# A hybrid decoder layer on one core: summed weights written over the raw ones, and another order of the gate/up steps

## The chip, the core and the metric

The kernel runs on one core of one Trainium2 chip. Time is the device time of one execution in microseconds (us); the number that counts is the median of several runs. The engines are TensorE (PE: matrix products, with weight loads shown apart as PEld), VectorE (DVE), ScalarE (ACT), GpSimd (POOL) and SyncE (SP, which here only starts transfers). Each has a queue of its own and takes its instructions strictly in the order in which they stand; an instruction whose input isn't ready holds up all that stands behind it on its engine.

## The reference

One decoder layer on 256 tokens of width 2048, all in float32:

```python
u = rmsnorm(h, ln1_w)
lru_x, lru_g, q, k, v, ret_g = split(u @ w_in)           # 2048 -> 6 x 1024
y = concat(rg_lru(conv(lru_x)) * gelu(lru_g), retention(q, k, v, ret_g))
h = h + y @ w_out                                         # 2048 -> 2048
u = rmsnorm(h, ln2_w)
ff = silu(u @ w_ffn_gate) * (u @ w_ffn_up)                # 2048 -> 5632, twice
h = h + ff @ w_ffn_down                                   # 5632 -> 2048
out = rmsnorm(h, final_norm_w)
```

The change lies in the last three lines, above all in `u @ w_ffn_gate` and `u @ w_ffn_up`.

## The kernel before

**Products in three parts.** Every float32 operand is split into a high part (rounded to the matrix engine's format, a copy on ACT, L102) and a low part (source minus high part, on DVE, L103). A product is then three matmuls: high by high, high by low, low by high (`three`, L656; the lines are L659, L660 and L661). The weights are split on the fly: a 128x1024 float32 tile `raw` (512 KB) is loaded, ACT writes `wh`, DVE writes `wl`, PE uses both. There are 5 `raw` buffers, and 4 each of `wh` and `wl`.

**A quad.** The gate/up weights come as quads: one quad is 256 rows of the left factor (two halves of 128, for two token tiles of 128: a11, a12, a21, a22) by a gate tile and an up tile of 512 columns (b11, b21 for gate, b12, b22 for up), in two loads: first half b11 and b12, second half b22 and b21. A plain quad costs eight products (`EIGHT`). A summed quad costs seven (`SEVEN`), Strassen's way, with weight sums t1 = b11 + b12, t2 = t1 + b22, t3 = b12 + b22, t4 = t2 + b21 on DVE, and sums s1 to s4 of the left factor made once (`Left`, L521). Results gather in PSUM banks c11, c21 (gate) and c12, c22 (up). There are two sets of four banks, `bank` and `aux`; column blocks take them in turn (`room`, L652).

**Column blocks.** Gate/up has 11 blocks j of 512 columns, each with 8 quads. In block 0 (`gate_up_first`) the quads numbered in SUMMED_FIRST are summed. In the blocks 1 to 10 (`gate_up`) the three quads numbered in SUMMED are worked in two steps, so that three of them share the additions on the results. A *shared* step, done while the block before is still running, computes the four products with b11, t2, t1, t3 into the banks of the next block; behind the last of the three, a few additions (L760 to L765, `p1`, `p`, `q`) mix those banks. A *direct* step, in its own block, loads the second half of the quad again and adds the three products with b21, t4 and b22; t4 is kept from the shared step. The other five quads are *plain* steps. So in steady state one block has five plain steps of 24 matmuls, three shared steps of 12 and three direct steps of 9: 183 matmuls and 19 loads.

**After a block** `ffn_post` (L811) applies the gate: tanh on ACT (L820), two products on DVE for each token tile (L821, L825), then eight transposes on PE (`turn`, L826, tile `ft`) and two copies on ACT to `ff`. `resid_tok` (L580) transposes the residual in some blocks (tile `ht`).

**Down** (`down_block`) has two blocks of 22 quads, five of them in each summed (SUMMED_DOWN) through the same `Quad.load`.

**What sets the order.** `program` is a list of steps; loads run three ahead of the step that needs them (AHEAD, L1067); `defer` puts late work off by a number of steps. That is the order in which the code is written; a list scheduler then sets the final order of each engine's queue when the kernel is built, and gives out the buffers. Queues are therefore fixed before the kernel runs.

## Time and profile before

| | |
|---|---|
| three runs | 1128.27, 1135.15, 1137.65 us; median 1135.15 |
| profiled execution | 1135.66 us; its span, first to last instruction, 1133.9 us |
| granted TensorE clock, mean | 0.996 |
| input projections, retention, output projection | 0 to about 388 us of the span |
| gate/up: block 0 | about 388 to 441 us |
| gate/up: blocks 1 to 10 | about 441 to 900 us |
| down and final norm | about 900 to 1134 us |

All positions below are microseconds from the start of the span of that one execution. In a row of the timeline stand the start, the time taken, the engine, the line of the kernel, the operation, output<-input, the size, how many, and in brackets the idle time of the engine just before it with what ended it. In a row of stretches stand, for each engine, busy microseconds and in brackets the number of instructions, then the granted clock, the share of the transfer engines' time, and GB/s. A matmul's recorded length overlaps the next one's: the distance between two starts is what one costs PE.

### The profile page before, as it was taken

To read this page: it belongs to the slowest core of one execution; us is meant where nothing else is said; L and a number is where in the kernel's file an instruction comes from. 1 tells how busy PE (TensorE), PEld (TensorE's weight loads), DVE (VectorE), ACT (ScalarE), POOL (GpSimd) and SP (SyncE) were. 2 spreads that over 40 slices of the span, in tenths; PEclk is the share of its full clock that TensorE was granted. 3 is DMA by queue.
4 is the path that set the end of the run, shared out by engine and by line. 5 is a ranking of instruction groups with operands and counts; after the bars stand their busy time and mean duration, and the time that the engine had idled before them with its cause. 6 is when DMAs were issued, how large, how long until landed. Compare 5 with 4: busy or idle time off the path is not lost.

```text
span 1133.9 us, 14754 instructions
## 1 busy us (share of the span) xinstructions
PE 1100.2 (97%) x5298; PEld 915.2 (81%) x5298; DVE 906.6 (80%) x1274; ACT 639.0 (56%) x877; POOL 57.4 (5%) x64
## 2 busy tenths in 40 slices
PE   9999999999999999999998999989999999999996
PEld 7888888888888977877876877767777888888885
DVE  7797799968777889778787787778876799777774
ACT  7766644478666556555555455554545665554553
POOL 0602220000000000000000000000000000020001
PEclk9999999999999999999999999999999999999999
DMA  9765565645655466667566575665757456746572
GB/s 326 236 196 167 177 232 168 196 156 169 215 192 186 146 208 241 217 211 240 196 231 228 176 239 182 234 223 184 246 186 256 160 183 209 245 140 219 199 240 76
DMA packets 66538, 230.47 MB, mean 203 GB/s; under 512 B 7584, under 2 KB 7968, under 8 KB 66464
## 3 DMA queue, kind: packets, MB, share of 16 engines
q1 hardware_dynamic: 65664, 227.43, 60.5%
q0 software_dynamic: 512, 1.57, 0.4%
q8 instruction: 41, 0.67, 0.2%
q10 hardware_dynamic: 288, 0.52, 0.1%
q14 instruction: 33, 0.27, 0.1%
HBM read 227.40 MB, written 2.10 MB: 202 GB/s over the span
## 4 chain that ended last, share of the span: by engine, by line
PE 60%; DVE 18%; DMA 15%; issue 4%; ACT 2%; DVEq 0%; SPq 0%; ACTq 0%
PE fm L143 15%; DMA raw<-in_w_gu 15%; DVE wl L103 10%; PE c L660 9%; PE c L661 8%; PE c L659 8%; PE fm L144 8%; PE tm L159 3%; PE tm L160 3%; PE tm L161 3%; ACT wh L102 2%; DVE raw L721 1%; DVE sum L717 1%; DVE raw L719 1%; PE p L659 1%
## 5 line engine op out<-in xcount | busy, mean ns | idle before, releaser
L103 DVE TENSOR_TENSOR wl<-raw,wh 128x1024 fp32r<-128x1024 f32 (+1 forms) x384 | 461.6, 1217 | 112.9 <-ACT wh L102 108.4
L102 ACT CAST wh<-raw 128x1024 fp32r<-128x1024 f32 (+1 forms) x384 | 390.4, 1032 | 274.2 <-DMA raw<-in_w_gu 60.3
L660 PE MATMUL c<-wl,ah 128*128 128x512 f32 x788 | 309.8, 395 | 14.8 <-DVE wl L103 14.7
L661 PE MATMUL c<-wh,al 128*128 128x512 f32 x788 | 306.7, 391 | 0.0
L659 PE MATMUL c<-wh,ah 128*128 128x512 f32 x788 | 261.4, 393 | 1.4 <-ACT wh L102 1.4
L660 PEld LDWEIGHTS c<-wl,ah 128*128 128x128 f32 x788 | 148.1, 188 | 53.8 <-DVE wl L103 24.3
L143 PE MATMUL fm<-u,wh 128*128 128x512 f32 x512 | 180.2, 396 | 0.0
L659 PEld LDWEIGHTS c<-wh,ah 128*128 128x128 f32 x788 | 147.8, 188 | 35.0 <-ACT wh L102 4.6
L661 PEld LDWEIGHTS c<-wh,al 128*128 128x128 f32 x788 | 148.1, 188 | 29.6
L144 PE MATMUL fm<-u,wl 128*128 128x256 f32 x512 | 144.1, 282 | 0.0
L102 ACT CAST wh<-sum 128x1024 fp32r<-128x1024 f32 x54 | 56.2, 1051 | 118.3 <-DVE sum L717 75.0
L143 PEld LDWEIGHTS fm<-u,wh 128*128 128x128 f32 x512 | 96.1, 188 | 22.0
L144 PEld LDWEIGHTS fm<-u,wl 128*128 128x128 f32 x512 | 97.0, 190 | 0.2
L143 PE MATMUL fm<-y,wh 128*128 128x512 f32 x224 | 78.8, 398 | 0.0
L103 DVE TENSOR_TENSOR wl<-sum,wh 128x1024 fp32r<-128x1024 f32 x54 | 65.3, 1222 | 6.4 <-ACT wh L102 6.2
L144 PE MATMUL fm<-y,wl 128*128 128x256 f32 x224 | 62.6, 281 | 0.0
L940 POOL TENSOR_TENSOR htok<-htok,fw 128x512 f32<-128x512 f32 (+1 forms) x7 | 10.9, 1573 | 934.2 <-ACT junk L938 934.2
L659 PE MATMUL c<-wh,sh 128*128 128x512 f32 x132 | 49.8, 403 | 5.8 <-ACT wh L102 5.5
L716 DVE TENSOR_TENSOR sum<-raw 128x512 f32<-128x512 f32 x30 | 20.7, 691 | 42.9 <-DMA raw<-in_w_gu 42.9
L660 PE MATMUL c<-wl,sh 128*128 128x512 f32 x132 | 52.1, 395 | 0.0
L661 PE MATMUL c<-wh,sl 128*128 128x512 f32 x132 | 52.0, 394 | 0.0
L143 PEld LDWEIGHTS fm<-y,wh 128*128 128x128 f32 x224 | 42.0, 188 | 10.0
(264 smaller groups left out, 1349.6 us busy)
## 6 DMA issues: line engine op xcount, KB each, us to landing
raw<-in_w_gu SPq DMA_DIRECT2D x206, 512.0 KB, 4.7
raw<-in_w_down SPq DMA_DIRECT2D x88, 512.0 KB, 4.4
raw<-in_w_out SPq DMA_DIRECT2D x32, 512.0 KB, 3.8
raw<-in_w_lx SPq DMA_DIRECT2D x16, 512.0 KB, 4.9
raw<-in_w_k SPq DMA_DIRECT2D x16, 512.0 KB, 3.7
raw<-in_w_q SPq DMA_DIRECT2D x16, 512.0 KB, 4.3
raw<-in_w_rg SPq DMA_DIRECT2D x16, 512.0 KB, 3.7
raw<-in_w_lg SPq DMA_DIRECT2D x16, 512.0 KB, 4.0
```

What stands on the lines that cost most here:

```text
L102: act.copy(out=dst_h, in_=src)
L103: v.tensor_tensor(out=dst_l, in0=src, in1=dst_h.bitcast(F32), op=ALU.subtract)
L143: pe.matmul(ps, wh, hl, start=first, stop=False)
L144: pe.matmul(ps[:, :S], wl, hl[:, :S], start=False, stop=last)
L159: pe.matmul(ps, ah, wh, start=first, stop=False)
L160: pe.matmul(ps, ah, wl, start=False, stop=False)
L161: pe.matmul(ps, al, wh, start=False, stop=last)
L659: pe.matmul(p, ah, bh, start=first, stop=False, skip_group_check=onto)
L660: pe.matmul(p, ah, bl, start=False, stop=False, skip_group_check=onto)
L661: pe.matmul(p, al, bh, start=False, stop=last, skip_group_check=onto)
L716: v.tensor_tensor(out=ta[:, :512], in0=b11, in1=b12, op=ALU.add)
L717: v.tensor_tensor(out=ta[:, 512:], in0=ta[:, :512], in1=b22, op=ALU.add)
```

## The change

**The sums are written over the raw weights.** A new function `add` puts t1 into the place of b11, t3 into that of b12, t2 into that of b22 and t4 into that of b21. The `sum` tiles, which took buffers of the `raw` pool (two for each summed quad, one for each shared step), are gone. Since b11, b22 and b21 are overwritten, they are split first where they are needed raw: in `Quad.load` the pair b22, b21 is split ahead of the sums; in `Shared.load` b11 is split as soon as the first half is there. The shared step's pairs change with that: b11 and t2 share one `wh`/`wl` pair, filled by two splits of 512 columns at different times, t1 and t3 share another, filled by one split of 1024. Before, t1 and t2, and b11 and t3, went together, in two splits of 1024.

**The steps of a block stand in another order.** Before, a block was: direct, direct, direct, plain, plain, shared, plain, shared, plain, shared, plain. Now: plain, plain, shared, direct, plain, shared, direct, plain, shared, direct, plain. The shared steps still belong to the next block.

**Smaller parts.** The quads worked in the Strassen way are now 2, 3 and 4 (before 1, 3 and 5), and in block 0 only quad 2 (before 1 and 3). A plain quad's eight products now start with the four that need only the first half; the last plain quad of a block keeps the old order, bank by bank. The seven of a summed quad start with the three that need no sum. The shared steps that run in block 0 come one step earlier, the residual's transposes are spread over blocks 1 to 4 in place of 1 and 2, and a block's transposes are put off by two steps in place of five and six, which puts them at about the same place, behind the first two plain steps of the next block.

```diff
-SUMMED = (1, 3, 5)
-SUMMED_FIRST = (1, 3)
+SUMMED = (2, 3, 4)
+SUMMED_FIRST = (2,)
...
         def load(self, half):              # Quad
...
+            self.cut(("b22", "b21"), r)
+            self.add(r)
+            self.cut(("t1", "t3"), self.ra)
+            self.cut(("t2", "t4"), r)
+
+        def add(self, r):
+
             b11, b12, b22, b21 = self.ra[:, :512], self.ra[:, 512:], r[:, :512], r[:, 512:]
-            ta, tb = (rpool.tile([P, 1024], F32, tag="raw", name=nm("sum")) for _ in range(2))
...
-            self.cut(("t1", "t2"), ta)
...
-            self.cut(("t3", "t4"), tb)
-            self.cut(("b22", "b21"), r)
+            for dst, a, b in ((b11, b11, b12), (b12, b12, b22), (b22, b11, b22), (b21, b22, b21)):
+                v.tensor_tensor(out=dst, in0=a, in1=b, op=ALU.add)
...
         def load(self, half):              # Shared
...
             if half == 0:
                 self.ra = r
+                h, l = self.hl = [wpool.tile([P, 1024], F32R, tag=g, name=nm(g)) for g in ("wh", "wl")]
+                self.parts["b11"] = h[:, :512], l[:, :512]
+                split(*self.parts["b11"], r[:, :512])
                 return
-            ra, ta = self.ra, rpool.tile([P, 1024], F32, tag="raw", name=nm("sum"))
...
+            self.add(r)
+            self.parts["t2"] = h[:, 512:], l[:, 512:]
+            split(*self.parts["t2"], r[:, :512])
+            self.cut(("t1", "t3"), self.ra)
             self.parts["t4"] = act_tile("t4h", F32R), act_tile("t4l", F32R)
-            split(*self.parts["t4"], b21)
+            split(*self.parts["t4"], r[:, 512:])
...
-        for m in range(len(SUMMED)):
-            quad = Direct(shared[j][m])
-            program.append(([quad], lambda m=m, quad=quad: direct(m, quad)))
         for n, i in enumerate(plain):
             quad = Quad(gu(j, i), False)
             program.append(([quad], lambda n=n, quad=quad: rest(n, quad)))
-            if n and n - 1 < len(ahead):
-                program.append(ahead[n - 1])
+            m = n - 1
+            if 0 <= m < len(SUMMED):
+                program.extend(ahead[m : m + 1])
+                quad = Direct(shared[j][m])
+                program.append(([quad], lambda m=m, quad=quad: direct(m, quad)))
```

What this makes of the queues is seen at three places of a block in the middle of gate/up.

**VectorE, the second shared step of a block, before.** `raw_1446` and `raw_1451` are the two halves of the shared quad, `raw_1438` and `raw_1443` those of the plain quad that is loaded ahead of it:

```order
L716 TENSOR_TENSOR sum_1452_7000<-raw_1446_6980 128x512
L717 TENSOR_TENSOR sum_1452_7000<-sum_1452_7000,raw_1451_6998 128x512
L719 TENSOR_TENSOR raw_1446_6980<-raw_1446_6980,raw_1451_6998 128x512
L721 TENSOR_TENSOR raw_1451_6998<-sum_1452_7000,raw_1451_6998 128x512
L103 TENSOR_TENSOR wl_1440_6940<-raw_1438_6937,wh_1439_6939 128x1024
L103 TENSOR_TENSOR wl_1445_6977<-raw_1443_6974,wh_1444_6976 128x1024
L103 TENSOR_TENSOR t4l_1458_7014<-raw_1451_6998,t4h_1457_7013 128x512
L103 TENSOR_TENSOR wl_1454_7004<-sum_1452_7000,wh_1453_7003 128x1024
L103 TENSOR_TENSOR wl_1456_7009<-raw_1446_6980,wh_1455_7008 128x1024
```

The same place now: `raw_1414` and `raw_1417` are the shared quad, `raw_1404` and `raw_1407` the plain quad loaded ahead of it, `raw_1422` the direct step's load:

```order
L103 TENSOR_TENSOR wl_1406_6941<-raw_1404_6938,wh_1405_6940 128x1024
L103 TENSOR_TENSOR wl_1409_6947<-raw_1407_6944,wh_1408_6946 128x1024
L103 TENSOR_TENSOR wl_1416_6969<-raw_1414_6966,wh_1415_6968 128x512
L641 TENSOR_TENSOR raw_1414_6966<-raw_1414_6966 128x512
L641 TENSOR_TENSOR raw_1414_6966<-raw_1414_6966,raw_1417_6981 128x512
L641 TENSOR_TENSOR raw_1417_6981<-raw_1414_6966,raw_1417_6981 128x512
L641 TENSOR_TENSOR raw_1417_6981<-raw_1417_6981 128x512
L103 TENSOR_TENSOR wl_1419_6990<-raw_1414_6966,wh_1418_6989 128x1024
L103 TENSOR_TENSOR wl_1424_7000<-raw_1422_6997,wh_1423_6999 128x1024
L103 TENSOR_TENSOR wl_1416_6969<-raw_1417_6981,wh_1415_6968 128x512
L103 TENSOR_TENSOR t4l_1421_6994<-raw_1417_6981,t4h_1420_6993 128x512
```

Before, the four sums, which need loads that come later, stood ahead of the two low-part splits of the plain quad; now every DVE instruction of this place stands in the order of the loads, but for the direct step's split, which stands ahead of that of t2.

**VectorE, the start of a block, before.** The first four splits here are those of the last plain step's second half and the three direct steps; `p`, `q`, `c22` and `c21` of L761 to L765 mix the banks, `gated` is the gate of the block that has just ended:

```order
L103 TENSOR_TENSOR wl_1479_7119<-raw_1477_7116,wh_1478_7118 128x1024
L103 TENSOR_TENSOR wl_1482_7125<-raw_1480_7122,wh_1481_7124 128x1024
L761 TENSOR_TENSOR p_1484_7141<-c12_1448_6986,p1_1483_7140 128x512
L103 TENSOR_TENSOR wl_1488_7152<-raw_1486_7149,wh_1487_7151 128x1024
L762 TENSOR_TENSOR q_1485_7142<-p_1484_7141,c22_1449_6990 128x512
L103 TENSOR_TENSOR wl_1491_7158<-raw_1489_7155,wh_1490_7157 128x1024
L764 TENSOR_TENSOR c22_1449_6990<-q_1485_7142,c21_1450_6994 128x512
L765 TENSOR_TENSOR c21_1450_6994<-c21_1450_6994,p_1484_7141 128x512
L821 SCALAR_TENSOR_TENSOR gated_1493_7168<-th_1492_7167,c11_1366_6621 128x512
L821 SCALAR_TENSOR_TENSOR gated_1495_7178<-th_1494_7177,c21_1369_6633 128x512
L103 TENSOR_TENSOR wl_1498_7198<-raw_1496_7195,wh_1497_7197 128x1024
```

Now the splits between the same additions are those of the first two plain quads (two halves each):

```order
L103 TENSOR_TENSOR wl_1453_7148<-raw_1451_7145,wh_1452_7147 128x1024
L767 TENSOR_TENSOR p_1449_7137<-c12_1411_6954,p1_1448_7136 128x512
L103 TENSOR_TENSOR wl_1456_7163<-raw_1454_7160,wh_1455_7162 128x1024
L768 TENSOR_TENSOR q_1450_7138<-p_1449_7137,c22_1412_6958 128x512
L103 TENSOR_TENSOR wl_1459_7169<-raw_1457_7166,wh_1458_7168 128x1024
L770 TENSOR_TENSOR c22_1412_6958<-q_1450_7138,c21_1413_6962 128x512
L771 TENSOR_TENSOR c21_1413_6962<-c21_1413_6962,p_1449_7137 128x512
L827 SCALAR_TENSOR_TENSOR gated_1461_7179<-th_1460_7178,c11_1332_6586 128x512
L827 SCALAR_TENSOR_TENSOR gated_1463_7189<-th_1462_7188,c21_1335_6598 128x512
L103 TENSOR_TENSOR wl_1466_7209<-raw_1464_7206,wh_1465_7208 128x1024
```

Splits that each feed 9 matmuls have been replaced by splits that each feed 12.

**TensorE, the first shared step of a block, before.** `wh_1434`, `wl_1435` hold b11 and t3, `wh_1432`, `wl_1433` hold t1 and t2; the banks with 144x are the next block's:

```order
L659 MATMUL c11_1447_6982<-wh_1434_6928,ah_663_3413 128x512
L659 MATMUL c12_1448_6986<-wh_1432_6923,sh_666_3422 128x512
L660 MATMUL c11_1447_6982<-wl_1435_6929,ah_663_3413 128x512
L661 MATMUL c11_1447_6982<-wh_1434_6928,al_664_3414 128x512
L660 MATMUL c12_1448_6986<-wl_1433_6924,sh_666_3422 128x512
L661 MATMUL c12_1448_6986<-wh_1432_6923,sl_667_3423 128x512
L659 MATMUL c22_1449_6990<-wh_1432_6923,sh_666_3422 128x512
```

Now `wh_1390`, `wl_1391` hold b11 and t2, `wh_1397`, `wl_1398` hold t1 and t3, and `wh_1402` is the direct step's:

```order
L661 MATMUL c11_1410_6950<-wh_1390_6850,ah_684_3524 128x512
L662 MATMUL c11_1410_6950<-wl_1391_6851,ah_684_3524 128x512
L663 MATMUL c11_1410_6950<-wh_1390_6850,al_685_3525 128x512
L661 MATMUL c21_1335_6598<-t4h_1321_6540,ah_684_3524 128x512
L662 MATMUL c21_1335_6598<-t4l_1322_6541,ah_684_3524 128x512
L663 MATMUL c21_1335_6598<-t4h_1321_6540,al_685_3525 128x512
L661 MATMUL c11_1332_6586<-wh_1402_6910,ah_684_3524 128x512
L661 MATMUL c12_1333_6590<-wh_1402_6910,sh_687_3533 128x512
L661 MATMUL c12_1411_6954<-wh_1390_6850,sh_687_3533 128x512
L661 MATMUL c22_1412_6958<-wh_1397_6900,sh_687_3533 128x512
L662 MATMUL c22_1412_6958<-wl_1398_6901,sh_687_3533 128x512
```

The products of b11 and t4, which need no sum of this step, have moved ahead; those of the direct step are mixed in; the first product of t2 stands ahead of those of t1 and t3.

39 lines of the change are left out of this document (16 added, 23 removed).

## The prediction, made before the changed kernel was run

> **What bounds the kernel now.** I read the page's busy times first, then stretches by stage, then counts, waits and timeline of the gate/up stage.
>
> ```profile
> PE 1100.2 (97%) x5298; PEld 915.2 (81%) x5298; DVE 906.6 (80%) x1274; ACT 639.0 (56%) x877; POOL 57.4 (5%) x64
> ...
> 388.00:441.00 53.00, 51.42 (x224) 40.15 (x222) 44.83 (x61) 29.30 (x33) 0.00 (x0) 1.00 0.67 224
> 430.00:441.00 11.00, 10.12 (x46) 7.51 (x44) 8.92 (x11) 6.40 (x8) 0.00 (x0) 1.00 0.88 314
> 441.00:530.00 89.00, 88.39 (x406) 72.54 (x406) 73.44 (x87) 52.79 (x66) 0.00 (x0) 1.00 0.66 220
> 530.00:865.00 335.00, 314.13 (x1368) 250.48 (x1368) 262.16 (x304) 173.76 (x202) 0.00 (x0) 0.99 0.64 214
> 900.00:1100.00 200.00, 200.00 (x884) 165.75 (x883) 162.26 (x192) 109.11 (x129) 7.64 (x4) 1.00 0.62 206
> ```
>
> PE looks full at 97%, but the stages differ. Down (900 to 1100) has no gap: nothing can be won there. Gate/up from 530 to 865 has 335 − 314.13 = 20.9 us of visible gaps, and more is hidden, since a recorded matmul overlaps the next one:
>
> ```profile
> 615.41 0.39 PE L661 MATMUL c<-wh,al 128*128 128x512 f32 x1
> ...
> 619.04 0.39 PE L661 MATMUL c<-wh,al 128*128 128x512 f32 x1
> ...
> 737.56 0.39 PE L659 MATMUL c<-wh,sh 128*128 128x512 f32 x1
> 737.79 0.39 PE L660 MATMUL c<-wl,sh 128*128 128x512 f32 x1
> 738.01 0.39 PE L661 MATMUL c<-wh,sl 128*128 128x512 f32 x1
> 739.11 0.50 PE L660 MATMUL c<-wl,ah 128*128 128x512 f32 x1 [0.70 <-DVE wl L103]
> ...
> 458.21 0.44 PE ft L832 x4
> ```
>
> The first two rows are 16 matmuls apart, 3.63 / 16 = 0.227 us from start to start where nothing is late; by the last, of the chain, four transposes take 0.44, 0.11 each. The gap at 739.11 is 1.10 from start to start and shown as 0.70. So the true work of the stretch can be counted, from the instructions at the three lines and the transposes (L659, L660, L661, L832, in this order):
>
> ```profile
> 530.00:865.00 335.00, 143.36 (x439) 81.53 (x439) 0.99 0.64 214
> 530.00:865.00 335.00, 173.62 (x437) 82.56 (x437) 0.99 0.64 214
> 530.00:865.00 335.00, 170.81 (x436) 82.35 (x436) 0.99 0.64 214
> 530.00:865.00 335.00, 9.51 (x56) 7.20 (x56) 0.99 0.64 214
> ```
>
> 1312 × 0.227 + 56 × 0.11 = 304.0 us, so **31.0 us are lost** there. At 183 matmuls a block that is 7.17 blocks: 46.7 us for each, of which 42.4 are work and 4.3 are stall. What PE waits for, and what those wait for:
>
> ```profile
> ACT wh L102 <- DMA raw<-in_w_gu: 49.5, 36, 3.2
> DVE sum L716 <- DMA raw<-in_w_gu: 37.7, 14, 3.9
> ...
> ACT wh L102 <- PE c L661: 15.4, 10, 4.4
> PE c L660 <- DVE wl L103: 13.6, 18, 1.2
> DVE sum L717 <- DMA raw<-in_w_gu: 12.9, 13, 2.0
> ...
> PE c L659 <- ACT wh L102: 6.2, 8, 1.4
> ```
>
> PE waits for splits; ACT and DVE wait for loads, DVE for 50.6 us at the first two sums alone. It isn't the volume: the core moves 214 GB/s here and took 314 between 430 and 441. A load waits for its buffer, and a late load holds a queue. This is one such place, the second shared step of a block (DVE, then ACT):
>
> ```profile
> 733.70 2.02 ACT L102 CAST wh<-raw 128x1024 fp32r<-128x1024 f32 x2 [2.85 <-issue]
> 733.72 0.69 DVE L716 TENSOR_TENSOR sum<-raw 128x512 f32<-128x512 f32 x1 [1.98 <-DMA raw<-in_w_gu]
> 736.02 0.69 DVE L717 TENSOR_TENSOR sum<-sum,raw 128x512 f32<-128x512 f32 x1 [1.61 <-DMA raw<-in_w_gu]
> 736.63 0.68 DVE L719 TENSOR_TENSOR raw<-raw,raw 128x512 f32<-128x512 f32 x1
> 737.23 0.68 DVE L721 TENSOR_TENSOR raw<-sum,raw 128x512 f32<-128x512 f32 x1
> 737.83 2.35 DVE L103 TENSOR_TENSOR wl<-raw,wh 128x1024 fp32r<-128x1024 f32 x2
> ```
>
> ACT has both high parts of the plain quad ready at 735.7. DVE was idle for 3.6 us, waiting with the sums for the shared quad's loads, and the plain quad's low parts stand behind them until 737.83: PE's 0.70 us at 739.11. The other place is a block's start:
>
> ```profile
> 762.73 0.50 PE L659 MATMUL c<-wh,ah 128*128 128x512 f32 x1 [0.57 <-ACT wh L102]
> 763.99 0.49 PE L660 MATMUL c<-wl,ah 128*128 128x512 f32 x1 [0.76 <-DVE wl L103]
> 765.72 0.50 PE L660 MATMUL c<-wl,ah 128*128 128x512 f32 x1 [0.77 <-DVE wl L103]
> ...
> 766.78 1.28 DVE L821 SCALAR_TENSOR_TENSOR gated<-th,c 128x512 f32<-128x512 f32 x2
> 769.10 1.41 DVE L825 SCALAR_TENSOR_TENSOR gated<-c,r_sq,gated 128x512 f32<-128x512 f32 x2
> ```
>
> Three direct steps follow each other there while DVE also mixes the banks and gates the old block.
>
> **The change part by part.** DVE's prices, start to start, from the rows above: 0.60 us for 512 columns (736.63 to 737.23), 1.13 for 1024 (2.35 for two, the last one 1.22 long).
>
> *Shared splits.* Two splits of 1024 become one of 1024 and two of 512: 2 × 0.60 − 1.13 = +0.07 us on DVE for each of 30 shared steps, 2 us in all, beside DVE's 335 − 262.16 = 73 us of idle time in this stretch. I cost it at nothing; without that cover it is +2 us. The Trainium skill (Perfetto Trace Analysis, Optimizing Scalar/DVE Operations) speaks for larger operations if the engine is saturated, with about 60 ns of overhead per DVE operation; by it the 30 extra ones would be an estimated 1.8 us. No such saturation stands in the row.
>
> *Buffers.* A block takes 22 `raw` buffers now (19 loads, 3 sums) and 19 afterwards, from the same 5. Within 42.4 us that allows each to be held 5 × 42.4 / 19 = 11.2 us in place of 9.6. Holding needs the load, cast, split and queueing; loads take 4.9 us:
>
> ```profile
> raw<-in_w_gu SPq DMA_DIRECT2D x136, 512.0 KB, 4.9
> ...
> 599.43 7.74 DMA raw<-in_w_gu
> ```
>
> *Order of DVE's queue.* The plain quad's splits now stand ahead of the shared quad's sums, so the 3.6 us at 733 hold up nothing that is already loaded. What waits behind the second sum now, the direct step's split among it, is loaded later anyway.
>
> *Order of the steps.* Before, a plain and a shared step together had 4 × 1.13 + 5 × 0.60 = 7.5 us of DVE beside 36 × 0.227 = 8.2 of PE (92%), three times in a row; the block's start had three splits (3.4), four bank operations (2.4) and four gating ones (about 2.6, from 1.28 and 1.41), 8.4 us beside 27 × 0.227 = 6.1 of PE (137%). Now plain, shared, direct: 4 × 1.13 + 7 × 0.60 = 8.7 beside 45 × 0.227 = 10.2 (86%), and the start has two plain steps: 4.5 + 2.4 + 2.6 = 9.5 beside 48 × 0.227 = 10.9 (87%). That overload is what stalls at 762 to 766. Five more loads per 10.2 us are 2.62 MB, 257 GB/s, under the 314 seen. SP's queue issues as many loads as before; POOL does nothing here.
>
> *Eight products, first half first.* Removes a wait for the second load's split, adds none; its gain is inside the 4.3 us.
>
> *Block 0.* One summed quad fewer: one product more, 3 × 0.227 = +0.7 us on PE. Its own visible gap is 53 − 51.42 = 1.6 us; I keep it, at bounds of nothing and 3 us for the earlier shared steps.
>
> *Down.* The same sums in place, with t2 and t4 now split last. PE has no gap and DVE 38 us spare of 200, so nothing. If PE had no lead, one summed quad would wait for four sums and two splits (2.4 + 2.3) less three products (2.0), 2.7 us, ten times: +27 at the worst. No row shows such a wait.
>
> *Transposes.* The residual's are as many; those of `ft` keep their place.
>
> *What is late next.* In the shared step PE now meets t2's first product ahead of t1's and t3's, and ACT writes t2's high part behind those of t1, t3 and the direct step. And the slack of 1.4 us in a group (10.2 − 8.7) does not cover a 7.7 us load, of which there was about one in a block. So stalls do not vanish. For the stall left per block the rows bound me: 0.3 (441 to 530: 89 − 88.39 over two blocks, when work was still ahead) and today's 4.3. I take 1.2, nearer to the first since DVE no longer is over 100% anywhere.
>
> Sum: 1135.66 − 31.0 + 7.17 × 1.2 + 0.7 = **1114.0** for an execution like the profiled one; the median of the runs lay 0.5 lower, so 1113.5, say 1113.
>
> *The clock.* The stall of 31.0 includes one slow patch, right behind three stalls (620.5 to 623.5):
>
> ```profile
> 623.52 0.50 PE L660 MATMUL c<-wl,ah 128*128 128x512 f32 x1 [0.77 <-DVE wl L103]
> 624.63 0.63 PE L660 MATMUL c<-wl,sh 128*128 128x512 f32 x1
> 625.06 0.63 PE L661 MATMUL c<-wh,sl 128*128 128x512 f32 x1
> ```
>
> Starts are 0.43 apart there, for seven matmuls: 1.4 us. I take it that this goes with the stalls. The Trainium skill (TensorE: Matmul & The Clock Gate, HAM oscillation) warns only of idle gaps over some 3.4 us. The gaps here are 0.8 us at most, so by that rule the patch is not their doing and could stay, which would make 1115.
>
> **The rivals.**
>
> *Half of it stays.* One family of stalls goes (the block's start), the shared steps keep theirs through t2 and the late loads: about 2.8 us a block. 1135.66 − 31.0 + 20.1 + 0.7 = 1125.5. For it: the order of t2; the load of 7.7 us. Against: DVE's queue order, which made the 733 stall, is mended.
>
> *Loads bind, and nothing moves.* If the 4.9 us per load come from the memory side, the same 19 loads take the same 46.7 us a block; with +0.7 and 2 us of DVE on the path: 1138. For it: ACT and DVE wait most for DMA. Against: the 314 GB/s. The Trainium skill (SBUF — State Buffer, A bandwidth-pool intuition that's wrong) calls HBM almost always the bottleneck end to end, and gives about 358 GB/s per core; the 314 seen agrees with that ceiling, and 257 would be under it.
>
> *Slower: the four split pairs.* The pair with b11 and t2 is now taken when the first half lands and freed behind t2's last product: by hand about 10 us (cast 0.5, 1.7 for the second load at 314 GB/s, sums 2.4, splits 1.1, 1.1 and 0.6, ten matmuls 2.3), where the other four of a group are held about 5.4 each (cast 1.0, split 1.1, some 14 matmuls 3.2). Sum 31.6 / 4 = 7.9 us per group, under 10.2. Casts already wait for PE to free a pair (15.4 us above). From 41 us on it binds; if each is held 3.3 us longer than by hand, the group takes 48.1 / 4 = 12.0 and a block 3 × 12.0 + 11.8 (two plain steps 10.9, eight transposes 0.9) = 47.8, 1.1 more than now over ten blocks: 1135.66 + 11 + 0.7 = 1147.
>
> **How the numbers follow.** My forecast (1103 to 1121, the low end with every counted stall gone and 2 us of those before 530 too) has 0.60; half 0.16; loads 0.16; split pairs 0.08. About 1%, 11 us, is what a measurement of this kernel can tell: faster means below 1123.8, slower above 1146.5. The forecast and half of the second case are faster, 0.68; the other half and the third are the same, 0.24; the last is slower, 0.08. Range 1101 to 1135: it takes in the forecast, the second case and the lower part of the third (which spreads some 5 us about 1138), and leaves out the rest of it and the last.
>
> **What would show it.** In the changed profile: the 441-to-900 stage ends some 20 us earlier; a block takes about 43.6 us; DVE's waits for loads at the in-place sums fall well under 50 us; no run of three stalls at a block's start; 900 to 1100 of the old profile still without gaps. I am wrong if PE still waits for `wl` about 18 times in seven blocks (loads or t2), if `wh` waits for PE grow far above 15 us (split pairs), or if gaps appear in down.

## The result

The changed kernel takes **1101.73 us** (median of 4 runs, 1100.82 to 1103.44) against 1134.08 us before (4 runs, 1128.27 to 1137.65): a ratio of 0.9721, with a 95% interval of 0.9678 to 0.9765. The forecast was 1113 us, within 1101 to 1135; the time lies 0.7 us inside the lower end of that range.

The profiled execution took 1100.82 us, with a span of 1099.0 us at a mean clock of 0.997. These are the busy line and the chain of waits of its page:

```profile
PE 1086.4 (99%) x5301; PEld 914.7 (83%) x5301; DVE 913.1 (83%) x1298; ACT 638.6 (58%) x905; POOL 57.2 (5%) x64
...
PE 97%; DVE 1%; DMA 0%; ACT 0%; issue 0%; SPq 0%; DVEq 0%; ACTq 0%
```

TensorE (PE) was busy 97% of the span before and is busy 99% of it now. VectorE (DVE) has more to do than before (906.6 us then), so nothing was gained by sparing it. The stretches of the prediction, and two more towards the end (from-to, length, busy time of PE, PEld, DVE, ACT and POOL with their instructions, granted clock, DMA share, GB/s):

```profile
388.00:441.00 53.00, 52.28 (x232) 42.68 (x231) 50.93 (x74) 32.77 (x42) 0.00 (x0) 1.00 0.66 223
441.00:530.00 89.00, 89.00 (x413) 74.01 (x412) 75.51 (x92) 50.52 (x66) 0.00 (x0) 1.00 0.68 230
530.00:865.00 335.00, 335.00 (x1522) 277.56 (x1521) 287.98 (x348) 193.05 (x249) 0.00 (x0) 1.00 0.69 229
865.00:900.00 35.00, 35.00 (x156) 28.78 (x155) 32.05 (x48) 21.36 (x27) 0.00 (x0) 1.00 0.53 180
900.00:1080.00 180.00, 179.22 (x791) 148.09 (x790) 137.08 (x153) 92.28 (x109) 6.24 (x4) 1.00 0.60 196
```

From 530 to 865 PE is busy for 335.00 of 335 us (314.13 before), with DVE at 86%. The count of true work says the same. These are the instructions of that stretch at the three matmul lines and at the two lines of transposes (L661, L662, L663, L838, L584, in this order):

```profile
530.00:865.00 335.00, 147.73 (x479) 89.60 (x479) 1.00 0.69 229
530.00:865.00 335.00, 183.94 (x479) 89.93 (x479) 1.00 0.69 229
530.00:865.00 335.00, 184.47 (x478) 89.78 (x479) 1.00 0.69 229
530.00:865.00 335.00, 10.77 (x72) 8.89 (x72) 1.00 0.69 229
530.00:865.00 335.00, 1.61 (x14) 1.26 (x12) 1.00 0.69 229
```

1436 × 0.227 + 86 × 0.11 = 335.4 us of work in 335 us: nothing is lost, where 31.0 us were. In the same time PE does 1436 matmuls in place of 1312. What is waited for there (engine, line, released by what: total us, times, longest):

```profile
ACT wh L102 <- DVE raw L641: 54.1, 19, 4.0
ACT wh L102 <- PE c L663: 52.8, 34, 5.1
DVE wl L103 <- ACT wh L102: 42.6, 48, 2.3
ACT wh L102 <- DMA raw<-in_w_gu: 14.8, 17, 1.8
...
DVE raw L641 <- DMA raw<-in_w_gu: 2.1, 2, 1.2
...
PEld c L661 <- ACT wh L102: 0.3, 2, 0.2
```

No wait of PE is listed for this stretch any more, and of its weight loads 0.3 us. DVE's waits for loads at the in-place sums (L641) are 2.1 us where the two sums of before had 50.6. ACT's wait for PE to free a split pair has grown from 15.4 to 52.8 us: ACT and DVE are now ahead and wait for PE. One place, the start of a block and its first shared step, on DVE:

```profile
647.75 0.68 DVE L767 TENSOR_TENSOR p<-c,p 128x512 f32<-128x512 f32 x1
...
654.21 1.22 DVE L103 TENSOR_TENSOR wl<-raw,wh 128x1024 fp32r<-128x1024 f32 x1
655.34 1.41 DVE L831 SCALAR_TENSOR_TENSOR gated<-c,r_sq,gated 128x512 f32<-128x512 f32 x2
658.69 0.69 DVE L103 TENSOR_TENSOR wl<-raw,wh 128x512 fp32r<-128x512 f32 x1 [1.93 <-ACT wh L102]
659.41 0.69 DVE L641 TENSOR_TENSOR raw<-raw 128x512 f32<-128x512 f32 x1
```

Bank additions, splits and gating run through without a wait, and DVE then idles 1.93 us ahead of the split of b11 (658.69). That idle spot turns out below to be the margin of this kernel. PE at the time of the old 0.70 us gap:

```profile
737.65 0.39 PE L662 MATMUL c<-wl,ah 128*128 128x512 f32 x1
...
741.96 0.39 PE L661 MATMUL c<-wh,ah 128*128 128x512 f32 x1
```

These are 19 matmuls apart, 4.31 / 19 = 0.227 us. In the median a load takes longer than before (5.3 us from issue to landing, 4.9 before), though the long ones have become rare (over 7 us: 2 of 137, before 18 of 136), and nobody on the path sees it:

```profile
raw<-in_w_gu SPq DMA_DIRECT2D x137, 512.0 KB, 5.3
```

For the comparison of all runs I use one number that is worked out from a trace: over all matmuls, the distance from one start to the next less the usual one of its width (0.227 us for 512 columns, 0.117 for 256, 0.109 for 128). I call the sum the stall; it includes short spells at half pace. What is left of the span is then, by definition, every matmul at its usual distance, with the start and the end of the span.

| kernel | time, us | ratio to before, 95% | span | stall in all | 388–530 | 530–865 | 865–900 | from 900 | span less stall |
|---|---|---|---|---|---|---|---|---|---|
| before | 1134.08 | 1 | 1133.9 | 49.1 | 5.4 | 31.4 | 0.1 | −0.3 | 1084.8 |
| after | 1101.73 | 0.9721 [0.9678, 0.9765] | 1099.0 | 13.5 | 1.3 | 0.1 | 0.1 | 0.9 | 1085.5 |
| e1 sums in place alone | 1111.17 | 0.9771 [0.9745, 0.9798] | 1112.5 | 27.9 | 5.2 | 6.7 | 4.0 | 0.5 | 1084.6 |
| e2 order of steps alone | 1125.49 | 0.9893 [0.9864, 0.9922] | 1123.0 | 38.2 | 7.0 | 19.4 | 0.0 | −0.3 | 1084.8 |
| e3 before, sixth raw buffer | 1119.98 | 0.9860 [0.9823, 0.9898] | 1125.6 | 40.6 | 4.8 | 17.3 | 0.1 | 5.2 | 1085.0 |
| e4 after, old order of eight | 1102.15 | 0.9695 [0.9673, 0.9718] | 1100.5 | 15.0 | 1.4 | 0.0 | 1.3 | 0.3 | 1085.5 |
| e5 e1 and e2 together | 1104.95 | 0.9707 [0.9670, 0.9745] | 1102.4 | 17.6 | 4.3 | 0.0 | 1.6 | 0.2 | 1084.8 |
| e6 after, four raw buffers | 1130.54 | 0.9926 [0.9905, 0.9947] | 1130.5 | 45.1 | 9.0 | 18.1 | 0.0 | 6.3 | 1085.4 |
| e7 after, DVE +1.2 us per shared step | 1126.21 | 0.9892 [0.9859, 0.9924] | 1123.2 | 37.7 | 5.1 | 19.1 | 0.0 | 2.1 | 1085.5 |
| e8 after, DVE +2.4 us per shared step | 1150.46 | 1.0096 [1.0061, 1.0131] | 1142.8 | 57.4 | 10.7 | 32.1 | 2.6 | 0.9 | 1085.4 |
| e9 e7 with a fifth split pair | 1106.10 | 0.9731 [0.9709, 0.9753] | 1104.3 | 18.8 | 3.9 | 3.5 | 0.0 | −0.2 | 1085.5 |
| e10 as e7, but on data of its own | 1132.38 | 0.9956 [0.9940, 0.9972] | 1130.4 | 44.8 | 6.6 | 25.1 | 0.0 | 1.8 | 1085.6 |
| e11 after, DVE +3.6 us per block at the gating | 1111.94 | 0.9780 [0.9764, 0.9795] | 1111.5 | 25.9 | 1.6 | 6.3 | 5.9 | 0.9 | 1085.6 |
| e12 after, seven summed quads in down | 1109.37 | 0.9755 [0.9741, 0.9770] | 1107.5 | 24.7 | 1.3 | 0.1 | 1.9 | 9.3 | 1082.8 |

The stages leave out the time up to 388 us, which holds 11 to 13 us of stall in every kernel. The ratios are to runs of the kernel before on the same chip, whose median lay between 1134.1 and 1139.5 us in the four groups of runs; small differences between times of different groups are better read from the ratio or from the stall. The last column shows only that the kernels do the same work: 1084.8 us before and 1085.5 after, the product more of block 0 (3 × 0.227 = 0.7 us). So the gain lies in the distances between matmuls: 49.1 − 13.5 = 35.6 us of stall less, 0.7 us of work more, 34.9 us between the two spans. The traced execution of e3 is its slowest, 7 us above its median, and that of e8 its fastest, 6 us below; their stalls are to be read with that in mind.

### The profile page after: what moved, and what is told of

The parts are those of the page before. It is cut to its first block, busy times and chain, and to the rows that moved or that the text cites. A ratio compares the mean times of both kernels' runs of the same rounds, so it can differ in the third digit from the quotient of the medians.

```text
span 1099.0 us, 14809 instructions
## 1 busy us (share of the span) xinstructions
PE 1086.4 (99%) x5301; PEld 914.7 (83%) x5301; DVE 913.1 (83%) x1298; ACT 638.6 (58%) x905; POOL 57.2 (5%) x64
## 4 chain that ended last, share of the span: by engine, by line
PE 97%; DVE 1%; DMA 0%; ACT 0%; issue 0%; SPq 0%; DVEq 0%; ACTq 0%
PE c L662 20%; PE c L663 20%; PE c L661 20%; PE fm L143 16%; PE fm L144 8%; PE tm L159 3%; PE tm L160 3%; PE tm L161 3%; PE p L661 1%; PE p L663 1%; PE p L662 1%; PE ft L838 1%; DMA x<-in_x 0%; DVE wl L103 0%; PE fm L150 0%; PE fm L148 0%
## 5 line engine op out<-in xcount | busy, mean ns | idle before, releaser
L102 ACT CAST wh<-raw 128x1024 fp32r<-128x1024 f32 (+1 forms) x467 | 447.5, 981 | 364.2 <-PE c L663 111.7
L103 DVE TENSOR_TENSOR wl<-raw,wh 128x1024 fp32r<-128x1024 f32 (+1 forms) x467 | 526.3, 1149 | 120.7 <-ACT wh L102 116.5
L662 PE MATMUL c<-wl,ah 128*128 128x512 f32 x794 | 308.8, 390 | 0.8 <-DVE wl L103 0.8
L663 PE MATMUL c<-wh,al 128*128 128x512 f32 x794 | 309.3, 390 | 0.0
L661 PE MATMUL c<-wh,ah 128*128 128x512 f32 x794 | 254.9, 391 | 0.4 <-ACT wh L102 0.4
L662 PEld LDWEIGHTS c<-wl,ah 128*128 128x128 f32 x794 | 149.0, 188 | 31.8 <-DVE wl L103 1.2
L661 PEld LDWEIGHTS c<-wh,ah 128*128 128x128 f32 x794 | 149.0, 188 | 31.1 <-ACT wh L102 0.9
L663 PEld LDWEIGHTS c<-wh,al 128*128 128x128 f32 x794 | 149.1, 188 | 30.7
L641 DVE TENSOR_TENSOR raw<-raw,raw 128x512 f32<-128x512 f32 x82 | 56.7, 691 | 4.4 <-DMA raw<-in_w_gu 2.1
L641 DVE TENSOR_TENSOR raw<-raw 128x512 f32<-128x512 f32 x82 | 56.7, 691 | 2.3
L662 PE MATMUL c<-wl,sh 128*128 128x512 f32 x131 | 51.0, 389 | 0.0
L663 PE MATMUL c<-wh,sl 128*128 128x512 f32 x131 | 51.0, 389 | 0.0
L161 PE MATMUL tm<-wh,u 128*128 128x512 f32 x128 | 48.8, 390 | 0.0
L160 PE MATMUL tm<-wl,u 128*128 128x512 f32 x128 | 48.7, 392 | 0.0
```

The lines of the kernel that those rows point to most:

```text
L102: act.copy(out=dst_h, in_=src)
L103: v.tensor_tensor(out=dst_l, in0=src, in1=dst_h.bitcast(F32), op=ALU.subtract)
L160: pe.matmul(ps, ah, wl, start=False, stop=False)
L161: pe.matmul(ps, al, wh, start=False, stop=last)
L641: v.tensor_tensor(out=dst, in0=a, in1=b, op=ALU.add)
L661: pe.matmul(p, ah, bh, start=first, stop=False, skip_group_check=onto)
```

## The experiments

The question is not whether the change helps but which part of it removes which stall, why what was expected to remain doesn't, and how much margin there is behind a full PE.

**One part alone: the sums in place.** The kernel before with the sums written over the raw halves, the shared quad's pairs (b11, t2) and (t1, t3), and the splits of b22 and b21 ahead of the sums; old positions, orders and steps.

```diff
-            ta, tb = (rpool.tile([P, 1024], F32, tag="raw", name=nm("sum")) for _ in range(2))
...
+            for dst, a, b in ((b11, b11, b12), (b12, b12, b22), (b22, b11, b22), (b21, b22, b21)):
+                v.tensor_tensor(out=dst, in0=a, in1=b, op=ALU.add)
```

> The kernel before with one part of the change alone: the sums written over the raw weights, and the shared step's pairs as in the change (b11 with t2, t1 with t3). The order of the steps, the quads chosen and the order of the eight products stay as before. Theory B (buffers and VectorE's queue: 19 takes of the 5 raw buffers in a block in place of 22, and the plain quad's splits no longer behind the shared quad's sums) has this part bring most of the gain: the stall at the second shared step goes, that at a block's start shrinks, 1105 to 1115 us. Theory S (order of the steps: three direct steps in a row under VectorE's bank additions and gates, 137% there) has the block's start still stall by about 2.4 us a block: 1118 to 1126 us. If neither the buffers nor the queue mattered, 1134 us.

Measured: 1111.17 us (1108.37 to 1114.27), ratio 0.9771. The stall from 530 to 865 falls from 31.4 to 6.7 us. What is left there are PE's gaps at the start of a block, for instance:

```profile
571.92 0.50 PE L661 MATMUL c<-wl,ah 128*128 128x512 f32 x1 [0.48 <-DVE wl L103]
573.25 0.50 PE L660 MATMUL c<-wh,sh 128*128 128x512 f32 x1 [0.36 <-ACT c L766]
```

(L661 is the low-part matmul in this kernel.) So this part carries most of the gain: 49.1 − 27.9 = 21.2 of the 35.6 us. No gap is left at the shared steps, and most of the stall at the block's start is gone. The edit does two things at once: it takes three buffers per block off the pool, and it puts DVE's queue in the order of the loads. The run with a sixth buffer, below, parts the two. Another 4.0 us have appeared at 865 to 900, at the passage into down.

**The other part alone: the order of the steps.** The kernel before with two plain steps ahead, then shared, direct and plain in turn, with the deferred transposes and the residual's moved as in the change; old sums, orders of products and positions.

```diff
...
-        for m in range(len(SUMMED)):
-            quad = Direct(shared[j][m])
-            program.append(([quad], lambda m=m, quad=quad: direct(m, quad)))
...
+            m = n - 1
+            if 0 <= m < len(SUMMED):
+                program.extend(ahead[m : m + 1])
+                quad = Direct(shared[j][m])
+                program.append(([quad], lambda m=m, quad=quad: direct(m, quad)))
```

> The kernel before with the other part alone: plain, plain, then shared, direct, plain in turn (with the transposes put off as in the change), the sums still in buffers of their own. Theory S: the block's start is free, most of the gain comes, 1105 to 1115 us. Theory B: 22 takes of 5 buffers in a block stay, and loads stay late; the stall moves to the shared steps, 1120 to 1134 us.

Measured: 1125.49 us (1121.29 to 1128.05), ratio 0.9893. The gaps at the block's start go, but for two of about 0.25 us; those at the shared steps stay (19.4 us from 530 to 865). The waits of this stretch, and one of the gaps:

```profile
ACT wh L102 <- DVE sum L717: 60.8, 20, 5.3
DVE sum L716 <- DMA raw<-in_w_gu: 44.4, 15, 4.1
```

```profile
605.90 0.50 PE L660 MATMUL c<-wl,ah 128*128 128x512 f32 x1 [1.57 <-DVE wl L103]
```

The sums still wait for their loads, 44.4 us at the first of them alone, and the splits behind them come late. By size and place this is the rival "half of it stays". By cause it isn't: that rival took the order of DVE's queue for mended and blamed t2's product, and here it is the queue that stalls. The order of the steps needs the other part.

**Is it the buffers alone?** The kernel before with six raw buffers in place of five (one activation tile fewer).

```diff
-    apool = ctx.enter_context(tc.tile_pool(name="acts", bufs=58))
+    apool = ctx.enter_context(tc.tile_pool(name="acts", bufs=57))
-    rpool = ctx.enter_context(tc.tile_pool(name="raw", bufs=5))
+    rpool = ctx.enter_context(tc.tile_pool(name="raw", bufs=6))
```

> The kernel before with six raw buffers in place of five (and 57 in place of 58 general tiles, which makes the room), nothing else. 22 takes of 6 buffers are about what 19 of 5 are. It parts the two halves of theory B: if the number of buffers alone is what held the loads, this comes to 1105 to 1115 us; if it is the place of the sums ahead of the plain quad's splits in VectorE's queue, which stays here, or the order of the steps, 1122 to 1134 us.

Measured: 1119.98 us (1118.19 to 1127.33), ratio 0.9860, between the two ranges that were expected. A sixth buffer removes the block-start stalls, and not those at the shared steps. One of these, DVE and PE in order of time:

```profile
602.55 0.69 DVE L716 TENSOR_TENSOR sum<-raw 128x512 f32<-128x512 f32 x1 [4.88 <-DMA raw<-in_w_gu]
603.16 1.22 DVE L103 TENSOR_TENSOR wl<-raw,wh 128x1024 fp32r<-128x1024 f32 x1
604.30 0.68 DVE L717 TENSOR_TENSOR sum<-sum,raw 128x512 f32<-128x512 f32 x1
604.44 0.50 PE L660 MATMUL c<-wl,ah 128*128 128x512 f32 x1 [1.31 <-DVE wl L103]
```

DVE stands idle for 4.88 us with a sum whose load is late, and only behind that does it make the split for which PE waits at 604.44. A load that is late for its own sum does no harm; the order of DVE's queue turns it into a stall of the plain step. Nor are the buffers too few here: six of them with 22 takes allow 6 × 42.4 / 22 = 11.6 us per hold, more than the 11.2 of the changed kernel, and 17.3 us of stall stay. So the in-place sums work in two ways, through the buffers and through the queue, and the queue is the part that a buffer can't replace.

**Both parts together, without the new orders of products and positions.** The kernel of the change with the old SUMMED, SUMMED_FIRST, EIGHT and SEVEN, and with block 0's shared steps at their old place.

```diff
-SUMMED = (2, 3, 4)
-SUMMED_FIRST = (2,)
+SUMMED = (1, 3, 5)
+SUMMED_FIRST = (1, 3)
...
-            for c, a, b in EIGHT if n < len(plain) - 1 else LAST:
+            for c, a, b in EIGHT:
```

> The kernel before with both large parts, sums in place and the order of the steps, but with the old quads (1, 3, 5; 1 and 3 in block 0), the old order of the eight and of the seven products. If the two parts are all of it, as the run with the old order of the eight suggests, this comes to 1100 to 1104 us (0.7 us of it the product saved in block 0). If the choice of the quads and the seven products' order carry part of the gain that the in-place run lacks, 1105 to 1110 us.

Measured: 1104.95 us (1104.18 to 1106.00), ratio 0.9707, on the border of the two ranges that were expected. From 530 to 865 no stall is left; the two parts do all of it. The rest of the change is seen in the stall of 388 to 530 (4.3 us here, 1.3 in the changed kernel) and of 865 to 900 (1.6 against 0.1), less 0.7 us for the additional product. That is 3 to 4 us by the traces; the ratios, with intervals of some 0.4% to each side, don't separate the two kernels.

**The eight products, first half first.** The changed kernel with the old order of the eight products.

```diff
-            todo += [(i, *e, 0, 512) for e in (SEVEN if q.sums else EIGHT if i < len(quads) - 1 else LAST)]
+            todo += [(i, *e, 0, 512) for e in (SEVEN if q.sums else LAST)]
...
-            for c, a, b in EIGHT if n < len(plain) - 1 else LAST:
+            for c, a, b in LAST:
```

> The changed kernel with the old order of the eight products in every plain quad, bank by bank, so that the second product already needs the second half. Theory: with the loads no longer late, this order is worth little, 1102 to 1105 us. If the four products of the first half are what covers a late second load, about 0.9 us for each of the two first plain steps of a block comes back as stall: 1112 to 1122 us.

Measured: 1102.15 us (1102.00 to 1103.68), ratio 0.9695; stall from 530 to 865 0.0 us. The order of the eight products is worth nothing in the blocks: with DVE and ACT ahead, the second half's split is there before either order asks for it. At 865 to 900, at down's first summed quads, this trace has 1.3 us of stall where the changed kernel has 0.1; the times don't tell the two kernels apart.

**How much do the buffers matter now?** The changed kernel with four raw buffers.

```diff
-    rpool = ctx.enter_context(tc.tile_pool(name="raw", bufs=5))
+    rpool = ctx.enter_context(tc.tile_pool(name="raw", bufs=4))
```

> The changed kernel with four raw buffers in place of five. 19 takes of 4 within 42.4 us leave 8.9 us for each; by the loads' 5.3 us and a cast, a split and some queueing that is just too little. Theory B: the stalls come back, some 2 us a block, 1115 to 1130 us. If five were far more than enough, 1102 us.

Measured: 1130.54 us (1128.12 to 1132.53), ratio 0.9926, half a us above the range that was expected: nearly all of the gain is lost. The waits from 530 to 865:

```profile
ACT wh L102 <- DMA raw<-in_w_gu: 58.4, 46, 2.7
...
PE c L662 <- DVE wl L103: 6.3, 10, 0.8
```

ACT waits 58.4 us for loads (14.8 in the changed kernel) and PE for splits again. With 19 takes, four buffers allow 4 × 42.4 / 19 = 8.9 us per hold and five 11.2; what this order of work needs lies between the two. Whether the 9.6 us of the kernel before would have been enough for it was not measured.

**How much room does DVE have?** The changed kernel with two, then four more 512-column subtractions in each shared step. They write the low part of t4 again with the same values.

```diff
+            th, tl = self.parts["t4"]
+            for _ in range(2):
+                v.tensor_tensor(out=tl, in0=r[:, 512:], in1=th.bitcast(F32), op=ALU.subtract)
```

> The changed kernel with VectorE's low part of t4 computed three times in each shared step in place of once (same result): 2 x 0.60 us more of VectorE in each of 30 shared steps. A group of plain, shared and direct step then has 8.7 + 1.2 = 9.9 us of VectorE beside 10.2 of TensorE (97%). If idle time of VectorE is all that decides, the time stays at 1102 to 1104 us; if its queue needs slack for late loads, a few tenths of a us for each shared step come back, 1107 to 1115 us.

> The same with four extra subtractions in each shared step: 8.7 + 2.4 = 11.1 us of VectorE beside 10.2 of TensorE in a group, and per block 36 + 7.2 = 43.2 beside 42.4. VectorE is then the bound: per block at least 0.8 us, within the three groups 0.9 each unless the two plain steps at the start make it good; 1110 us at the least (nine blocks at 0.8 us), 1128 us if each group stalls for itself.

Measured: 1126.21 us (1125.23 to 1127.56), ratio 0.9892, for two, and 1150.46 us (1144.64 to 1153.30), ratio 1.0096, for four. I had expected at most 1115 us of two and at most 1128 of four; both were misses. The additional work is 30 × 2 × 0.60 = 36 us in all, 3.6 us per block, and with it come 19.1 us of stall from 530 to 865, about 2.6 us per block (7.4 blocks of 45.2 us), though DVE idled (335 − 287.98) / 7.9 = 5.9 us per block in the changed kernel. The stretch from 530 to 865 with two, and with four:

```profile
530.00:865.00 335.00, 323.93 (x1435) 259.27 (x1434) 295.70 (x370) 181.79 (x232) 0.00 (x0) 1.00 0.64 219
```

```profile
530.00:865.00 335.00, 314.80 (x1367) 245.52 (x1365) 310.79 (x405) 175.28 (x226) 0.00 (x0) 1.00 0.64 212
```

With two, DVE is busy only 88% of the time and yet PE loses 19 us. Where it idles, in the same kernel's timeline (ACT, then DVE, then PE), and ACT's main wait of that stretch:

```profile
671.76 0.62 ACT L102 CAST wh<-raw 128x512 fp32r<-128x512 f32 x1 [7.02 <-PE c L663]
672.42 0.69 DVE L103 TENSOR_TENSOR wl<-raw,wh 128x512 fp32r<-128x512 f32 x1 [4.03 <-ACT wh L102]
676.88 0.50 PE L661 MATMUL c<-wh,ah 128*128 128x512 f32 x1 [0.90 <-ACT wh L102]
```

```profile
ACT wh L102 <- PE c L663: 59.9, 32, 7.0
```

Ahead of the first shared step ACT waits 7.02 us until PE frees a split pair, DVE idles 4.03 us behind it, and then, from the shared steps on, DVE has no gap over 0.34 us until the next block's gating is done. The step's four sums can only follow (the first at 673.14), since b11 has to be split before t1 is written over it; ACT's further casts come behind the sums, and PE waits 0.90 us for one of them. Some 7.9 us of the stall are lost at this place, and 6.9 at the blocks' start, where the additions on the banks come late. DVE could use those 4 us to work ahead only if it had a pair to write to. This gave a new theory: **the four split pairs cap how far ACT and DVE can get ahead**, so idle time in one part of the block can't pay for work in another. Three runs test it.

**A fifth split pair under the same load.** The kernel with two more subtractions, five pairs, three activation tiles fewer.

```diff
-    apool = ctx.enter_context(tc.tile_pool(name="acts", bufs=58))
+    apool = ctx.enter_context(tc.tile_pool(name="acts", bufs=55))
-    wpool = ctx.enter_context(tc.tile_pool(name="split", bufs=4))
+    wpool = ctx.enter_context(tc.tile_pool(name="split", bufs=5))
```

> The changed kernel with two more 512-column subtractions per shared step, as in the run that took 1126.2 us, and with five split pairs in place of four (three fewer tiles among the activations). Theory 1, the four pairs cap how far DVE can work ahead: with a fifth pair the wait of ACT for a pair that PE frees (59.9 us between 530 and 865 in that run) shrinks to under 30 us and the time falls by half of the 24 us or more, to 1102 to 1114. Theory 2, what costs is that the extra work holds the raw buffers and with them the loads longer: a fifth pair changes nothing, 1122 to 1130, and ACT's wait turns into one for loads. Theory 3, DVE as a whole has no room: the same 1122 to 1130, with DVE's idle time where it was.

Measured: 1106.10 us (1105.27 to 1108.74), ratio 0.9731. The same additional work now costs 18.8 − 13.5 = 5.3 us of stall in place of 24.2. The stretch from 530 to 865, ACT's waits in it, and DVE's wait at a block's first shared step:

```profile
530.00:865.00 335.00, 332.80 (x1504) 274.51 (x1503) 306.54 (x383) 189.96 (x241) 0.00 (x0) 1.00 0.68 229
```

```profile
ACT wh L102 <- DVE raw L641: 68.4, 19, 5.8
ACT wh L102 <- PE c L663: 41.7, 37, 4.3
```

```profile
665.28 3.50 DVE L103 TENSOR_TENSOR wl<-raw,wh 128x1024 fp32r<-128x1024 f32 x3 [1.25 <-ACT wh L102]
```

DVE now does 306.54 us of work in 335, 92%, and PE is all but full; its wait there is 1.25 us. ACT's longest wait for a pair is 4.3 us in place of 7.0; its sum of 41.7 us is above the 30 that were expected, because some of that wait is there whenever ACT is ahead. DVE's room as a whole is not the limit, and neither is the number of raw buffers, which is the same. The scheduler has also used the fifth pair to set another queue: b11 is now split ahead of the gating, and the first sum (658.12) stands among its instructions, where with four pairs both came behind it. More lead and the other order come together here; no run parts them.

**The same DVE time on data of its own.** Two operations per shared step that read only the parts of t4 and write a tile of their own.

```diff
+            junk = act_tile("junk")
+            for _ in range(2):
+                v.tensor_tensor(out=junk, in0=th.bitcast(F32), in1=tl.bitcast(F32), op=ALU.subtract)
```

> The changed kernel with two more 512-column DVE operations per shared step that read only the two parts of t4 and write a tile of their own: as much DVE time as in the run of 1126.2 us (36 us over 30 shared steps), but no raw buffer is held for it and no product waits for its result. Theory 1 (the place in the group is what counts, because the lead is capped): still 1118 to 1128, since the splits behind it in DVE's queue come as late. Theory 2 (the raw buffers held longer): 1102 to 1108.

Measured: 1132.38 us (1130.93 to 1133.05), ratio 0.9956. No raw buffer is held for these operations and no product waits for their result, and they cost still more, 31.3 us of stall. So it is the place in DVE's queue that costs. From 530 to 865 both runs lose some 7.9 us at the first shared steps; at the blocks' start this one loses 12.3 us, that with the subtractions 6.9. Why, and so why the time lies above the range that was expected, stays open.

**The same DVE time at another place.** From the second block on, six additions per block beside the gating, into a tile of their own.

```diff
+                junk = act_tile("junk")
+                for _ in range(6 if j else 0):
+                    v.tensor_tensor(out=junk, in0=gated[1], in1=gated[1], op=ALU.add)
```

> The changed kernel with six more 512-column DVE additions per block beside the gating (a tile of their own, the output is not touched), from the second block on: 3.6 us per block, as much as two per shared step. Theory 1 (slack is local: DVE idles 2.1 us per block just before the first shared step, and the gating lies just ahead of that): about 1.5 us per block stick out, 10 blocks, 1104 to 1118, clearly under 1126. Theory 3 (DVE's total is what counts): the same as in the groups, 1122 to 1130.

Measured: 1111.94 us (1111.22 to 1113.32), ratio 0.9780. The stretches from 530 and from 865:

```profile
530.00:865.00 335.00, 332.92 (x1492) 271.13 (x1490) 307.85 (x382) 189.55 (x242) 0.00 (x0) 1.00 0.68 227
865.00:900.00 35.00, 32.66 (x134) 25.80 (x133) 32.26 (x51) 19.61 (x27) 0.00 (x0) 0.90 0.47 154
```

As much DVE time per block as with the two subtractions per shared step costs 6.3 us of stall from 530 to 865, not 19.1, since here it runs into the idle spot ahead of the first shared step. Another 5.9 us fall at 865 to 900, where the last block's gating stands in front of down. In the queue three of the six stand behind the gating and three between the sums of the first shared step. The same DVE time costs a third in the blocks and half in the whole kernel (25.9 − 13.5 = 12.4 us of stall against 24.2), by its place.

**Can down be shortened with the room that is left?** The changed kernel with seven summed quads in down, so that four products, 12 × 0.227 = 2.7 us, are saved.

```diff
-SUMMED_DOWN = (2, 5, 8, 11, 14)
+SUMMED_DOWN = (2, 4, 7, 9, 12, 14, 17)
```

> The changed kernel with seven summed quads of the down product in place of five (positions 2, 4, 7, 9, 12, 14, 17), so two groups of three products fewer for each half: four products, 12 matmuls of 0.227 us, 2.7 us less on PE, against four more sets of four sums and six splits of 512 columns or their equal on DVE, about 4 x 2.4 + 4 x 1.1 = 14 us beside 43 us that DVE idles between 900 and 1080. If DVE's idle time there can be used: 1099, ratio to the changed kernel 0.9975. If the lead is capped as in the gate/up blocks, so that closer summed quads stall PE: 1102 to 1110.

Measured: 1109.37 us (1108.73 to 1109.85), ratio 0.9755: slower than the changed kernel, by the spans 8.5 us. The work did shrink (span less stall 1082.8, 2.7 less), but the stall grew by 24.7 − 13.5 = 11.2. The worst place, on PE:

```profile
993.84 0.50 PE L661 MATMUL p<-wh,sh 128*128 128x512 f32 x1 [2.15 <-ACT wh L102]
995.29 1.22 PE L661 MATMUL p<-wh,sh 128*128 128x512 f32 x2 [0.95 <-ACT wh L102]
996.31 0.63 PE L661 MATMUL c<-wh,ah 128*128 128x512 f32 x1
996.74 0.63 PE L662 MATMUL p<-wl,sh 128*128 128x512 f32 x1
```

This is at the start of down's second half: the sums of two summed quads stand close together in DVE's queue (six of the eight from 990.83 to 998.69), and PE waits 2.15 and 0.95 us for their casts. DVE idles 43 us of the 180 in the changed kernel's down, and again that isn't room that can be used. No run has a shorter time than the changed kernel; e4 and e5 have lower ratios, but the three intervals overlap.

## Why the prediction was right, and where it wasn't

**Sign, place and mechanism held.** The gain is stall of gate/up (31.4 us to 0.1 from 530 to 865, 5.4 to 1.3 from 388 to 530), and it comes from the two places that were named and from a third: of the 6.2 us that PE waited for `wh` by the prediction's list, 5.2 stood at a place it doesn't name, some 12 us ahead of a block's end, where a shared step's product waited for a cast of its sums. Alone, the in-place sums remove the stall at the shared steps, and the order of the steps that at the block's start; the waits of DVE at the sums fall from 50.6 to 2.1 us; the run of three gaps at a block's start is gone; with no stall left a block takes the 42.4 us of its work, and eight transposes or 0.9 us more where it holds the residual's, where 43.6 were forecast.

**That the range held is luck.** The time, 1101.73 us, lies below the forecast's own case of 1103 to 1121, whose low end had every counted stall gone and 2 us besides. It is inside the range by 0.7 us, and one of the four runs (1100.82) is outside.

**The residual stall was the term that was mis-sized.** I took 1.2 us per block, 8.6 us in all; measured are 0.1 us over the whole stretch. The argument was that a slack of 1.4 us in a group doesn't cover a load of 7.7 us. That step was wrong: a late load has to be covered by how far ACT and DVE are ahead when it comes, not by the slack of one group. Now 14.8 us of waits for loads on ACT, and one of 1.16 us on DVE at a shared step's sums (671.20), never reach PE. The long loads were not constant either, as the step had them: before, 18 took over 7 us, two or three in a block, and now 2 do. With 11.2 us per hold of a raw buffer the loads are issued early enough; with 8.9 (e6) they are not. The sum was 1114.0 for the profiled execution, 13.2 us too high: 8.9 from 530 to 865, 1.9 from 441 to 530, which I had left as it was, 2.3 in block 0, 1.2 up to 388, where the change does nothing, and −1.1 in down.

**Block 0.** Its own gap was kept at 1.6 us, with bounds of 0 and 3. The stall from 388 to 441 goes from 3.5 to 1.2 us, all of it in two gaps:

```profile
405.52 1.19 PE L661 MATMUL c<-wh,ah 128*128 128x512 f32 x4 [0.43 <-ACT wh L102]
407.00 0.73 PE L661 MATMUL c<-wh,sh 128*128 128x512 f32 x2 [0.28 <-ACT wh L102]
```

The visible gap is 0.72 us (53 − 52.28), inside the bounds. The additional product shows as three matmuls more (5301 for 5298), 0.7 us at their distance.

**Shared splits at nothing.** They cost nothing, but the cover that I named, "73 us of idle time", was no proof. In e7, 30 × 1.2 us in the same place cost 24 us while DVE still idled 39.3 us in this stretch. What covers them, as far as the trace shows, is the 1.93 us ahead of the first shared step and small gaps in the groups. The result of that step was right, its reason wasn't. How much less than 1.2 us per shared step would be free was not measured.

**Eight products.** "Its gain is inside the 4.3": in the blocks nothing of that gain is its own (e4).

**Down.** Costed at nothing, with 27 us at the worst if PE had no lead; measured 0.9 us, one gap. The mechanism of that worst case exists: in e12, with summed quads closer together, four more of them add 8.4 us from 900 on and 1.8 us ahead of it, 2.6 us each on average. That this is near the 2.7 that had been worked out for one without a lead is chance: half of it is lost at one place, half pace included.

**The clock.** In the changed kernel the granted clock from 530 to 865 is 1.00 (0.99 before), and the patch of 1.4 us is gone with the stalls, as taken. The Trainium skill (TensorE: Matmul & The Clock Gate, HAM oscillation) speaks of idle gaps over some 3.4 us; by that rule the patch could have stayed. In e12 there is such a patch again, right behind gaps of 2.15 and 0.95 us: starts 0.43 us apart from 995.9 to 998.4. In all the traces such patches of 512-column matmuls, after 388 us, stand only behind gaps, and all these gaps are shorter than the page's figure. The measurement decides: here gaps that short can be followed by half pace. But not all are, as the last section shows, so that the patch goes with the stalls was well taken but not certain.

**The rivals.** *Half of it stays* (1125.5) is what the order of steps gives alone (1125.49), for another cause (e2) and to the hundredth by chance; with both parts it didn't come about. *Loads bind* (1138): refuted, since with 229 GB/s and 5.3 us a load PE has no stall. The Trainium skill (SBUF — State Buffer, A bandwidth-pool intuition that's wrong) calls HBM almost always the bottleneck end to end; this trace doesn't agree, for a stretch with PE at 335.00 of 335 us is bound by PE. With a buffer fewer (e6) waits for loads do stall PE at 223 GB/s: what bound was the number of buffers, not the memory. *The four split pairs* (1147): ACT's wait for them grew from 15.4 to 52.8 us, which I had named as a sign that I was wrong. It wasn't one: ACT waited because it was ahead. But under more DVE work the pairs are the next limit, as e9 shows: of 24 us of stall with four pairs a fifth takes 19 away.

## What to carry to other kernels

Count the stall from start to start and give it to places before you edit; then ask of each place whether an in-order queue holds ready work behind work whose load is late, since that can be mended without any faster unit. The idle share of an engine is no margin: how much work it takes depends on where the work stands and on how many staging buffers let the engine get ahead, and adding work of no use at one place and at another measures it in two runs. A producer's growing wait for the consumer's buffers is a good sign as long as the consumer itself has no gaps.

## What the runs showed that I had not expected

TensorE's own pace didn't change with what the other engines did. From 530 to 865 us the median distance from one 512-column matmul to the next start is 0.227 us in all fourteen kernels, with DVE busy for 78% of the time (before) to 93% (e8) and loads at 212 to 231 GB/s.

Half pace follows short gaps, but not all of them. Behind gaps of 2.15 and 0.95 us seven matmuls in e12 started 0.43 us apart; in e11 twelve did at 880 us, behind gaps of 1.32 and 0.69 us, and the granted clock of 865 to 900 is 0.90. In e2 gaps of 1.13 and 0.48 us were enough (778 us), in e3 a single one of 1.96 us (409 us). Yet the three gaps at 762 to 766 us of the kernel before, shown in the prediction, are followed by no half pace, though three of much the same size at 620 to 624 us are; and in e10, with the two below and others like them in each block, the granted clock of 530 to 865 is 1.00.

```profile
574.51 0.50 PE L662 MATMUL c<-wl,ah 128*128 128x512 f32 x1 [0.75 <-DVE wl L103]
576.19 0.50 PE L661 MATMUL c<-wh,ah 128*128 128x512 f32 x1 [0.72 <-ACT c L773]
```

```profile
530.00:865.00 335.00, 319.28 (x1408) 254.39 (x1408) 291.54 (x367) 177.07 (x228) 0.00 (x0) 1.00 0.63 213
```

Neither the length of the gaps nor their number alone decides it, and what does was not found.
